# Linear attention in one trunk kernel: half roots of three heads on GpSimd in twelve operations, and output-projection weights from the fourth on split behind the last gates

## The chip, the cores and the metric

The kernel runs on one core of a Trainium2 chip. The metric is device time in microseconds (us): the median of three runs, beside one profiled execution whose trace is quoted throughout. The engines are named as the profile names them: PE is TensorE's matrix multiplies (PEld its weight loads), DVE is VectorE, ACT is ScalarE, POOL is GpSimd, SP is SyncE, which here only issues DMAs.

## What is computed

The reference is a decoder trunk of two layers over 512 tokens and 16 meta tokens, width 1024. Each layer is a feed-forward block, a token mixer, and a second feed-forward block. The mixer of layer 0 is gated linear attention with four heads; the change touches only it. Cut to what matters:

```python
q, k, v, r, lr = split(hn @ w_in)                  # 4 heads, keys 128 wide, values 256 wide
gk = log_sigmoid(lr @ w_gate + b_gate) / 16        # the forget gate
...                                                # chunks of 64: scan, attention, states
o = o_intra + einsum('bhncd,bhndv->bhncv', q_dec, states)
o = rmsnorm(o, g_head) * silu(r)                   # per head and token, over 256 values
return o @ w_out                                   # the output projection
```

## The kernel before

**Order of the work.** PE is the engine that everything is arranged around. A small planner (`Flow`) holds a clock and a heap of jobs. A job is a Python generator that gives out instructions and yields either an estimated delay or another job that it waits for; the main program advances the clock with every matmul that it writes (`mm`, `transpose`, L216). This fixes the order of PE by hand. The order on DVE, ACT and POOL is chosen when the kernel is built, by a scheduler that sees the same estimates and the dependencies. On the chip each engine then runs its own list strictly in order, with semaphores between engines.

**Weights.** Weights arrive as f32 in tiles called `raw` and are split in two parts, a high one made by ACT (L274 and L294, `w<-raw`) and a low one by DVE as a difference (L277 and L295, `w<-raw,w`). `split_unit` (L280) is the job for a plain unit: output projection, among others. Each split tile takes 128x512 on both engines. `L300` adds two raw tiles on DVE for Strassen's products.

**A head of linear attention** is one job, `core(h)`; between its pieces PE works on the input projections of the next head (`x<-x_l0m`), or, in head 2, on the products `a`, `c`, `d` of the gate projection, whose operands are the tiles `zl0m_t` (high part by ACT at L1005, low part by DVE at L1006). In order, a head does this:

- two scans on DVE, L1344 and L1345, from the log gates to `b`
- PE transposes the head's values `V` to tokens by values (`pv`, two groups of four, named pv_0 and pv_1 in the rows of the program's order); ACT copies them out (L1352)
- decays `d`, `f`, `c` (L1361 to L1371) on ACT and DVE, attention, states
- PE computes the output `po` for four blocks of 128 tokens and `pn` for the meta tokens
- ACT squares them and accumulates sums per token (L1434, L1436)
- `half_roots` (L476 to L489, called at L1439): ten DVE instructions on 128x5 numbers, from a sum to half an inverse square root, by an integer guess and two Newton steps. The tile is `half_go`
- ACT scales `po` by the roots, four times `on` (L1443) and once `onm` (L1444)
- PE transposes `on` back (`pt`, L216) and ACT copies the result into `V` (L1453)

The values `V` themselves are written by DVE from PE's projections (L1293, `V<-x,R_l0m`), one instruction of 128x272 and one of 128x256 for each half of a head's values.

**Gates.** Eight jobs `gated(m)` make the operands of the output projection: a tanh on ACT (L1464), two DVE instructions (L1466 and L1471), and `split` into `og`, the high part by ACT (L543) and the low part by DVE (L544). The loop over `plan` spawns them in four pairs. At its last pass but one it raises the cap on loads (`cap`, `prefetch`), and the jobs that split the output projection's eight weight units then run beside the gates. `out_proj` writes PE's products `y<-og,w`.

Of the kernel before, what the change touches and what calls it, by code (L numbers as in the profile page):

```python
# [11 lines left out]
I32 = mybir.dt.int32  # L12
AF = mybir.ActivationFunctionType
ALU = mybir.AluOpType
# [4 lines left out]
KD = 8  # L19
# [7 lines left out]
HEADS = 4  # L27
RSQRT_MAGIC = float(0x5F3759DF)
# [114 lines left out]
def trunk_kernel(ctx: ExitStack, tc, a, out, last_out):  # L143
    nc = tc.nc
    pe, act, dve, pool, sp = nc.tensor, nc.scalar, nc.vector, nc.gpsimd, nc.sync
    flow = Flow()
# [21 lines left out]
    def duo(name):  # L168
        t = pair_tile(name, F32)
        return t[:, 0], t[:, 1]  # L170
# [78 lines left out]
    used, asked, freed, ahead, cap, dma_end = [0], [0], [0], [16], [len(units)], [0.0]  # L249
# [2 lines left out]

    owed, chains = {}, [0]
    rooting, diagonal = set(), []
    building, last_sum, pair_behind, pauses = [], [], {}, []

    def set_ahead(n, slots=None):
        ahead[0], limit[0] = n, slots or n
# [3 lines left out]
    def slot(i):  # L262

        while live[0] + sum(n for j, n in owed.items() if j < i) >= limit[0]:
            yield room[0]
        live[0] += 1
        owed[i] -= 1
# [4 lines left out]
    def split_part(i, raw, m):  # L272
        w = pair_tile(f"w{i}_{len(loaded[i])}")
        high = act.activation(w[:, 0, :m], raw[:, :m], AF.Copy)  # L274
        for x in building:
            after(x.built, high)
        dve.tensor_tensor(w[:, 1, :m], raw[:, :m], w[:, 0, :m].bitcast(F32), op=ALU.subtract)  # L277
        loaded[i].append(w)

    def split_unit(i, raws):  # L280
        yield 2.2
        for raw, m in raws:
            while any((1, KD - 1) not in x.ready for x in building):
                yield 0.5
            yield from slot(i)
            split_part(i, raw, m)
# [50 lines left out]
    def load_unit():  # L337
# [34 lines left out]
        else:  # L372
# [6 lines left out]
            dma_end[0] = max(dma_end[0], flow.clock) + n * 1.5e-3  # L379
            loaded.append([])  # L380
            gen = split_unit(i, raws)
        split_jobs.append(flow.spawn(gen, dma_end[0] - flow.clock))

    def prefetch():
        while len(loaded) < cap[0] and asked[0] + costs[len(loaded)] <= freed[0] + ahead[0]:
            if isinstance(units[len(loaded)], list) and (chains[0] == CHAINS or rooting):
                break
            load_unit()
# [84 lines left out]
        return yy  # L473


    def half_roots(sums, dim, name):  # L476
        n = sums.shape[1]
        t = sm.tile([P, 4, n], F32, tag="half", name=f"half_{name}", bufs=2)
        aa, yy, zz, ww = (t[:, i] for i in range(4))
        dve.tensor_scalar(aa, sums, 1.0 / dim, 1e-6, op0=ALU.mult, op1=ALU.add)  # L480
        dve.tensor_scalar(yy.bitcast(I32), aa.bitcast(I32), -0.5, RSQRT_MAGIC, op0=ALU.mult, op1=ALU.add)
        dve.tensor_tensor(zz, yy, yy, op=ALU.mult)
        dve.tensor_tensor(zz, zz, aa, op=ALU.mult)
        dve.tensor_scalar(ww, zz, 0.375, -1.25, op0=ALU.mult, op1=ALU.add)
        dve.tensor_tensor(ww, ww, zz, op=ALU.mult)
        dve.scalar_tensor_tensor(yy, ww, 1.875, yy, op0=ALU.add, op1=ALU.mult)
        dve.tensor_tensor(zz, yy, yy, op=ALU.mult)
        dve.scalar_tensor_tensor(zz, zz, -0.25, aa, op0=ALU.mult, op1=ALU.mult)
        dve.scalar_tensor_tensor(yy, zz, 0.75, yy, op0=ALU.add, op1=ALU.mult)  # L489
        return yy  # L490

    def rstd(sq, n, dim, half, name, eng=pool, more=0.0):
# [114 lines left out]
    class Residual:  # L607
# [44 lines left out]
        def turn(self, g, sums):  # L652
# [22 lines left out]
            residual(0, 0)  # L675
            total(1)
            f = half_roots(st[:, : n // P], D, self.name)
            residual(0, 1)
            for c in cs:
# [306 lines left out]
    def bring_back_h(kept):  # L986
        H.fresh()
        for q in range(KD // 2):
            rows = slice(2 * q, 2 * q + 2)
            pool.dma_start(H[:, rows, kept], h_kept[:, rows, kept])  # L990
# [262 lines left out]
    def gla(x, finish):  # L1253
        set_ahead(10)
        with tc.tile_pool(name="gp", bufs=1) as gp:
# [82 lines left out]
            def core(h, before):  # L1338
# [86 lines left out]
                sums = sm.tile([P, 5], F32, tag="sums", name=f"sums{h}", bufs=2)  # L1425
# [10 lines left out]
                act.activation(onm, pm[:META, :256], AF.Square, accum_out=sums[:META, 4:5])  # L1436
                mids[h].finish(flow)
                yield SQUARED
                f = half_roots(sums, 256, f"go{h}")  # L1439
                yield DCHAIN  # L1440
                for b in range(4):
                    o = banks[b // 2][:, b % 2 * 256 : b % 2 * 256 + 256]
# [19 lines left out]
            def gated(m):  # L1462
                gs, th = rg[m]
                act.activation(th, gs, AF.Tanh, scale=0.5)  # L1464
                yield 0.8
                dve.scalar_tensor_tensor(gs, th, 1.0, gs, op0=ALU.add, op1=ALU.mult)  # L1466
                yield cores[m // 2]
                yield 0.8 + m % 2 * 1.5
                og[m] = pair_tile(f"og{m}")
                gn = vec[:, V_GN + m % 2 : V_GN + m % 2 + 1]  # L1470
                dve.scalar_tensor_tensor(gs, gs, gn, V[:, m], op0=ALU.mult, op1=ALU.mult)  # L1471
                split(og[m], gs, (0, TOK))
# [9 lines left out]
            for h in range(HEADS):  # L1482
                cores.append(flow.spawn(core(h, [gate] + late + mids[h - 1 : h])))
                if h == 1:
                    flow.spawn(right_factors(x, halves, z, plain, 1.2))
                if h + 1 < HEADS:
                    kk = [("k", h + 1), ("q", h + 1), ("v", 2 * h + 2), ("v", 2 * h + 3)]
                    if h + 2 == HEADS:
                        set_ahead(16, RING)
                        late = x_units(x, 3, L0, lambda i, g, p, kk=kk: evac(*kk[i], g, p))  # L1490
                        plain.finish(flow)
                        late += x_units(x, 1, L0, lambda i, g, p, kk=kk: evac(*kk[3], g, p))
                    else:
                        late = x_units(x, 4, L0, lambda i, g, p, kk=kk: evac(*kk[i], g, p))
            cap[0] = used[0] + len(GLA_PAIRS)
            tiles = Strassen(z, halves, 1)
            jobs = []

            def gating(m):
                rg[m], rg[m + 1] = duo(f"rg{m}"), duo(f"rg{m + 1}")  # L1500
                return Projected(tiles, rg[m][0], rg[m + 1][0])

            def finish_gates(m):
                jobs.extend([flow.spawn(gated(m)), flow.spawn(gated(m + 1))])

            plan = [(lambda m=m: gating(m), lambda m=m: finish_gates(m)) for m in range(0, KD, 2)]

            def begin(i):
                if i == len(plan):
                    return None  # L1510
                t = plan[i][0]()
                t.head()
                return t

            cur = begin(0)
            for i in range(len(plan)):
                cur.body()
                nxt = begin(i + 1)
                cur.tail()
                if i + 2 == len(plan):  # L1520
                    cap[0] = used[0] + KD
                    prefetch()
                plan[i][1]()
                cur = nxt
            bring_back_h(slice(0, TOK))
            flow.wait(*jobs[:6])
            set_ahead(16)
# [321 lines left out]
    x = nxt  # L1849
    nxt, fin = into("l0f1", 0, 3, False, lambda k: gain(0, 4, k), L0)  # L1850
    gla(x, fin)
    x = nxt
    nxt, fin = into("kv", 0, 5, True, lambda k: vec[:, V_KVN + k : V_KVN + k + 1], L0, (1, 1))
# [122 lines left out]
```

## Time and profile before

| | |
|---|---|
| median of 3 runs | 1848.33 us (1847.84 to 1848.58) |
| the profiled execution, its own time | 1847.98 us |
| its span in the trace | 1846.2 us |
| PE busy | 1832.8 us |
| DVE, ACT, POOL busy | 1482.9, 1140.2, 334.0 us |

The span runs from the first to the last recorded instruction; the profiled execution's own time lies 1.8 us above it. A busy row says how long an engine had an instruction in work, whether or not that instruction had to wait for a clock or a port. The rows of a timeline give the start in us from the span's start, the busy time, the engine, the line of the kernel, the operation, the tile written and the tiles read, the shape and the count, and in square brackets the idle time ahead of it with the instruction that ended that idle time. The view by windows gives busy time and count of each engine in a stretch of time, and under PEclk the clock granted to TensorE as a share of the full one. Linear attention's four heads end near 446, 475, 505 and 542 us; the last gates lie near 560 us.

### The profile page before, as it was taken

How to read it: one execution, taken by the hardware profiler on the slowest of the kernel's cores; microseconds unless marked ns; L12 is line 12 of the kernel's file. 1: busy time of each engine (PE TensorE's matmuls, PEld its weight loads, DVE VectorE, ACT ScalarE, POOL GpSimd, SP SyncE). 2: the span in 40 equal slices, each digit the busy share in tenths (PEclk: the TensorE clock that was granted, in tenths of full speed). 3: DMA queues.
4: the chain of work that ended last, by engine and by line, in shares of the span. 5: the costliest groups of instructions: out<-in, count | busy, mean ns of one | idle time of the engine just before them, and what ended most of it. 6: DMA issues, size and time to landing. Idle time of an engine off the chain costs nothing.

```text
span 1846.2 us, 38798 instructions
## 1 busy us (share of the span) xinstructions
PE 1832.8 (99%) x14696; PEld 1776.5 (96%) x14696; DVE 1482.9 (80%) x3047; ACT 1140.2 (62%) x2643; POOL 334.0 (18%) x499
## 2 busy tenths in 40 slices
PE   9999999999999999999999999999999999999998
PEld 9999999999899999999999899999987898999998
DVE  6889888678684788988878789898777678888884
ACT  6666666654566566665665566666667765666564
POOL 2210101321001411010133110212320042111122
PEclk9999999999999999999999999999999999999999
DMA  7756658434234365665853465759430226657681
GB/s 244 196 152 155 167 148 242 158 116 94 50 118 153 105 173 154 154 168 145 256 183 103 139 164 145 180 150 243 159 115 12 69 86 166 160 152 175 155 254 49
DMA packets 146251, 277.45 MB, mean 150 GB/s; under 512 B 16400, under 2 KB 36752, under 8 KB 146064
## 3 DMA queue, kind: packets, MB, share of 16 engines
q1 hardware_dynamic: 114208, 198.15, 33.5%
q0 software_dynamic: 31424, 76.23, 20.7%
q8 instruction: 115, 1.88, 0.4%
q14 instruction: 72, 0.59, 0.1%
q10 hardware_dynamic: 432, 0.59, 0.1%
HBM read 236.05 MB, written 38.34 MB: 149 GB/s over the span
## 4 chain that ended last, share of the span: by engine, by line
PE 91%; DVE 4%; ACT 2%; DMA 1%; issue 1%; SPq 0%; DVEq 0%; ACTq 0%
PE a L204 29%; PE x L204 17%; PE y L204 17%; PE c L204 14%; PE d L204 7%; PE o L204 1%; DVE w L295 1%; PE po L204 1%; ACT s L1696 1%; DVE w_s L295 1%; DMA H<-in_h 1%; DVE raw L300 1%; PE pt L216 1%; ACT w_s L294 0%; DMA raw<-in_w_in 0%
## 5 line engine op out<-in xcount | busy, mean ns | idle before, releaser
L295 DVE TENSOR_TENSOR w_s<-raw,w_s 128x512 fp32r<-128x512 f32 (+1 forms) x432 | 275.1, 647 | 78.8 <-ACT w_s L294 74.5
L294 ACT ACTIVATE w_s<-raw 128x512 fp32r<-128x512 f32 (+1 forms) x432 | 251.0, 593 | 93.0 <-DVE raw L327 49.1
L295 DVE TENSOR_TENSOR w<-raw,w 128x512 fp32r<-128x512 f32 (+1 forms) x324 | 204.2, 646 | 4.1
L353 POOL DMA_DIRECT2D raw<-in_w_in x112 | 104.6, 976 | 449.1 <-DVE w L295 100.5
L294 ACT ACTIVATE w<-raw 128x512 fp32r<-128x512 f32 (+1 forms) x324 | 185.1, 590 | 0.0
L277 DVE TENSOR_TENSOR w<-raw,w 128x512 fp32r<-128x512 f32 x232 | 153.9, 696 | 26.5 <-ACT w L274 24.5
L300 DVE TENSOR_TENSOR raw<-raw,raw 128x512 f32<-128x512 f32 (+1 forms) x264 | 168.0, 636 | 2.2
L274 ACT ACTIVATE w<-raw 128x512 fp32r<-128x512 f32 x232 | 134.5, 620 | 2.4 <-PE y L204 1.1
L204 PE MATMUL y<-hidl0f,w 128*128 128x272 f32 (+1 forms) x960 | 119.4, 285 | 0.0
L204 PEld LDWEIGHTS y<-hidl0f,w 128*128 128x128 f32 x960 | 118.0, 188 | 0.2
L204 PE MATMUL a<-zl0f_t,w_s 128*128 128x264 f32 x864 | 117.3, 285 | 0.0
L204 PE MATMUL y<-hidl1f,w 128*128 128x256 f32 (+1 forms) x768 | 114.9, 310 | 0.0
L204 PE MATMUL a<-zl1f_t,w_s 128*128 128x256 f32 x864 | 113.9, 281 | 0.0
L204 PEld LDWEIGHTS y<-hidl1f,w 128*128 128x128 f32 x768 | 104.9, 188 | 8.5
L538 POOL TENSOR_TENSOR acc_post<-acc_post,sq_post 128x256 f32<-128x256 f32 (+1 forms) x77 | 62.0, 805 | 273.7 <-ACT sq_post L537 270.2
L204 PEld LDWEIGHTS a<-zl0f_t,w_s 128*128 128x128 f32 x864 | 110.4, 188 | 0.0
L1250 POOL DMA_DIRECT2D kept_y<-dn x32 | 36.5, 1141 | 407.1 <-DVE w_s L295 165.3
L204 PEld LDWEIGHTS a<-zl1f_t,w_s 128*128 128x128 f32 x864 | 107.1, 188 | 0.0
L204 PE MATMUL x<-x_l0m,w 128*128 128x256 f32 (+1 forms) x768 | 102.2, 289 | 0.0
L204 PE MATMUL x<-x_l0f,w 128*128 128x256 f32 (+1 forms) x768 | 98.1, 287 | 1.4 <-ACT w L274 0.7
L204 PEld LDWEIGHTS x<-x_l0f,w 128*128 128x128 f32 x768 | 94.8, 189 | 2.7 <-DVE w L277 1.2
L204 PEld LDWEIGHTS x<-x_l0m,w 128*128 128x128 f32 x768 | 95.8, 188 | 1.6 <-issue 0.8
(593 smaller groups left out, 4255.4 us busy)
## 6 DMA issues: line engine op xcount, KB each, us to landing
raw<-in_w_in SPq DMA_DIRECT2D x408, 256.0 KB, 4.2
raw<-in_w_in POOLq DMA_DIRECT2D x112, 256.0 KB, 5.4
raw<-in_w_down SPq DMA_DIRECT2D x128, 192.0 KB, 2.4
raw<-in_gla_in SPq DMA_DIRECT2D x52, 256.0 KB, 3.6
raw<-in_w_last SPq DMA_DIRECT2D x48, 256.0 KB, 4.9
kept_y<-dn POOLq DMA_DIRECT2D x16, 528.0 KB, 8.2
raw<-in_w_out SPq DMA_DIRECT2D x32, 256.0 KB, 2.9
kept_y<-dn POOLq DMA_DIRECT2D x16, 512.0 KB, 8.7
```

The lines of the kernel that those rows point to most:

```text
L204: inst = pe.matmul(o, lhs, rhs, start=start, stop=stop, skip_group_check=onto)
L216: pe.transpose(o, src, ident)
L274: high = act.activation(w[:, 0, :m], raw[:, :m], AF.Copy)
L277: dve.tensor_tensor(w[:, 1, :m], raw[:, :m], w[:, 0, :m].bitcast(F32), op=ALU.subtract)
L294: act.activation(w[:, 0, :m], src, AF.Copy)
L295: dve.tensor_tensor(w[:, 1, :m], src, w[:, 0, :m].bitcast(F32), op=ALU.subtract)
L300: return dve.tensor_tensor(dst, dst, src, op=ALU.add)
L353: added = pool.dma_start(r, src, accum_op=ALU.add)
L538: pool.tensor_tensor(sums[0][:, :n], sums[0][:, :n], t[:, :n], op=ALU.add)
L1250: pool.dma_start(y_sum[:, 2 * self.q : 2 * self.q + 2, o : o + 2 * n], self.y[:, :, : 2 * n], accum_op=ALU.add)
L1696: act.activation(s[:, c], s[:, c], AF.Exp, scale=rc[:, c % 2 : c % 2 + 1], bias=nm[:, c : c + 1], accum_out=den[:, c : c + 1],)
```

## The change

The change has two parts, and both act only in the mixer of layer 0.

1. `half_roots` takes an engine. Heads 0, 1 and 2 pass GpSimd, head 3 still passes DVE. On GpSimd each of the three `scalar_tensor_tensor` steps becomes a `tensor_scalar` and a `tensor_tensor`, arranged so that there are twelve instructions instead of ten.
2. A dictionary `unit_behind` names units whose job waits for another job before it splits. When the cap for the output projection is raised, units 3 to 7 of its eight (the fourth on) are put behind a new job `gated_all`, which ends when all eight `gated` jobs have ended.

```diff
     def split_unit(i, raws):
         yield 2.2
+        if i in unit_behind:
+            yield unit_behind.pop(i)
         for raw, m in raws:
...
-    def half_roots(sums, dim, name):
+    def half_roots(sums, dim, name, eng=dve):
...
+        if eng is dve:
+            dve.scalar_tensor_tensor(yy, ww, 1.875, yy, op0=ALU.add, op1=ALU.mult)
+            dve.tensor_tensor(zz, yy, yy, op=ALU.mult)
+            dve.scalar_tensor_tensor(zz, zz, -0.25, aa, op0=ALU.mult, op1=ALU.mult)
+            dve.scalar_tensor_tensor(yy, zz, 0.75, yy, op0=ALU.add, op1=ALU.mult)
+        else:
+            eng.tensor_scalar(ww, ww, 1.875, None, op0=ALU.add)
+            eng.tensor_tensor(yy, yy, ww, op=ALU.mult)
+            eng.tensor_tensor(zz, yy, yy, op=ALU.mult)
+            eng.tensor_tensor(zz, zz, aa, op=ALU.mult)
+            eng.tensor_scalar(zz, zz, -0.25, 0.75, op0=ALU.mult, op1=ALU.add)
+            eng.tensor_tensor(yy, yy, zz, op=ALU.mult)
         return yy
...
-                f = half_roots(sums, 256, f"go{h}")
+                f = half_roots(sums, 256, f"go{h}", pool if h + 1 < HEADS else dve)
...
+            gated_all = Job(None)
+
+            def all_gated():
+                for j in jobs:
+                    yield j
+                gated_all.finish(flow)
...
                 if i + 2 == len(plan):
+                    unit_behind.update((j, gated_all) for j in range(used[0] + 3, used[0] + KD))
                     cap[0] = used[0] + KD
                     prefetch()
...
+            flow.spawn(all_gated())
             bring_back_h(slice(0, TOK))
```

The lines of the changed kernel stand ten further on behind `half_roots`: L1443 before is L1453 after, L1006 is L1016. The order of PE's 4255 rows and of SP's rows is the same in both programs, apart from names. POOL's list gains the 36 rows of the three chains, each at its head's place. DVE's list loses 30 rows; DVE and ACT lists are also re-sorted at a few places within linear attention, and nowhere else.

The first place is ACT in head 2. `on` and `onm` are the scalings that read the roots; `zl0m_t_6607` (6613 in the changed kernel) is the fourth of the gate projection's operand tiles of this stretch. Before:

```order
L1005 ACTIVATE zl0m_t_6584<-xsl0m_5737 128x528
L294 ACTIVATE w_11_6590<-raw_0_6520 128x512
L1005 ACTIVATE zl0m_t_6607<-xsl0m_5738 128x528
L1390 ACTIVATE dec_6832<-b_6631 128x4
L1352 ACTIVATE vt_6634<-pv_0_6635 128x4x128
L1361 ACTIVATE d_6682<-b_6631 128x528
L1443 ACTIVATE on_6493<-po_0_6490,half_go_6546 128x256 x2
L1443 ACTIVATE on_6493<-po_1_6491,half_go_6546 128x256 x2
L1444 ACTIVATE onm_6494<-pn_6492,half_go_6546 16x256
L1352 ACTIVATE vt_6634<-pv_1_6650 128x4x128
```

And in the changed kernel, where the five scalings have moved ahead of the fourth `zl0m_t`, of `dec`, of the copy of pv_0 and of `d`:

```order
L1015 ACTIVATE zl0m_t_6590<-xsl0m_5737 128x528
L296 ACTIVATE w_11_6596<-raw_0_6524 128x512
L1453 ACTIVATE on_6497<-po_0_6494,half_go_6550 128x256 x2
L1453 ACTIVATE on_6497<-po_1_6495,half_go_6550 128x256 x2
L1454 ACTIVATE onm_6498<-pn_6496,half_go_6550 16x256
L1015 ACTIVATE zl0m_t_6613<-xsl0m_5738 128x528
L1400 ACTIVATE dec_6838<-b_6637 128x4
L1362 ACTIVATE vt_6640<-pv_0_6641 128x4x128
L1371 ACTIVATE d_6688<-b_6637 128x528
```

The second place is DVE at the same time. `V_3<-x_0` and `V_3<-x_1` write the values that PE's pv_1 transposes. Before:

```order
L295 TENSOR_TENSOR w_11_6590<-raw_0_6520,w_11_6590 128x512
L483 TENSOR_TENSOR half_go_6546<-half_go_6546 128x5
L1006 SCALAR_TENSOR_TENSOR zl0m_t_6607<-xsl0m_5738,zl0m_t_6607 128x528
L484 TENSOR_SCALAR half_go_6546<-half_go_6546 128x5
L1344 SCALAR_TENSOR_TENSOR b_6631<-resets,ls_5498 128x528
L485 TENSOR_TENSOR half_go_6546<-half_go_6546 128x5
L1345 SCALAR_TENSOR_TENSOR b_6631<-resets,ls_5498 128x528
L486 SCALAR_TENSOR_TENSOR half_go_6546<-half_go_6546 128x5
L1293 TENSOR_TENSOR V_3_6532<-x_0_6535,R_l0m 128x272
L487 TENSOR_TENSOR half_go_6546<-half_go_6546 128x5
L1293 TENSOR_TENSOR V_3_6532<-x_1_6536,R_l0m 128x256
```

And in the changed kernel, where the fourth `zl0m_t` stands between the two scans and so ahead of both writes of `V_3`, and the addition of two raw tiles has moved up:

```order
L297 TENSOR_TENSOR w_11_6596<-raw_0_6524,w_11_6596 128x512
L302 TENSOR_TENSOR raw_0_6524<-raw_0_6524,raw_3_6527 128x512
L1354 SCALAR_TENSOR_TENSOR b_6637<-resets,ls_5498 128x528
L1016 SCALAR_TENSOR_TENSOR zl0m_t_6613<-xsl0m_5738,zl0m_t_6613 128x528
L1355 SCALAR_TENSOR_TENSOR b_6637<-resets,ls_5498 128x528
L1303 TENSOR_TENSOR V_3_6536<-x_0_6539,R_l0m 128x272
L1303 TENSOR_TENSOR V_3_6536<-x_1_6540,R_l0m 128x256
```

The third place is DVE at the last two gates. `og` are the gated values, `w_0` and `w_1` the halves of a unit of the output projection's weights. Before:

```order
L1471 SCALAR_TENSOR_TENSOR rg_7117<-rg_7117,vec,V_3_6532 128x528
L277 TENSOR_TENSOR w_0_7330<-raw_0_7179,w_0_7330 128x512
L277 TENSOR_TENSOR w_1_7333<-raw_512_7181,w_1_7333 128x512
L544 TENSOR_TENSOR og_7354<-rg_7116,og_7354 128x528
L277 TENSOR_TENSOR w_0_7358<-raw_0_7183,w_0_7358 128x512
L277 TENSOR_TENSOR w_1_7361<-raw_512_7185,w_1_7361 128x512
L277 TENSOR_TENSOR w_0_7376<-raw_0_7226,w_0_7376 128x512
L277 TENSOR_TENSOR w_1_7379<-raw_512_7228,w_1_7379 128x512
L544 TENSOR_TENSOR og_7385<-rg_7117,og_7385 128x528
```

And in the changed kernel, where both `og` follow the gates at once and the weights come behind them; ACT's list has the same shift:

```order
L1481 SCALAR_TENSOR_TENSOR rg_7123<-rg_7123,vec,V_3_6536 128x528
L554 TENSOR_TENSOR og_7354<-rg_7122,og_7354 128x528
L554 TENSOR_TENSOR og_7373<-rg_7123,og_7373 128x528
L277 TENSOR_TENSOR w_0_7377<-raw_0_7185,w_0_7377 128x512
L277 TENSOR_TENSOR w_1_7380<-raw_512_7187,w_1_7380 128x512
L277 TENSOR_TENSOR w_0_7383<-raw_0_7189,w_0_7383 128x512
```

More of the change, by code (lines that the diff above doesn't have):

```diff
@@ L254, in trunk_kernel @@
     rooting, diagonal = set(), []
-    building, last_sum, pair_behind, pauses = [], [], {}, []
+    building, last_sum, pair_behind, unit_behind, pauses = [], [], {}, {}, []
     def set_ahead(n, slots=None):
@@ L479, in half_roots @@
         aa, yy, zz, ww = (t[:, i] for i in range(4))
[L480 to L489, printed above, removed]
+        eng.tensor_scalar(aa, sums, 1.0 / dim, 1e-6, op0=ALU.mult, op1=ALU.add)
+        eng.tensor_scalar(yy.bitcast(I32), aa.bitcast(I32), -0.5, RSQRT_MAGIC, op0=ALU.mult, op1=ALU.add)
+        eng.tensor_tensor(zz, yy, yy, op=ALU.mult)
+        eng.tensor_tensor(zz, zz, aa, op=ALU.mult)
+        eng.tensor_scalar(ww, zz, 0.375, -1.25, op0=ALU.mult, op1=ALU.add)
+        eng.tensor_tensor(ww, ww, zz, op=ALU.mult)
+        if eng is dve:
[6 more added lines that the diff above has]
+            eng.tensor_tensor(yy, yy, ww, op=ALU.mult)
+            eng.tensor_tensor(zz, yy, yy, op=ALU.mult)
+            eng.tensor_tensor(zz, zz, aa, op=ALU.mult)
+            eng.tensor_scalar(zz, zz, -0.25, 0.75, op0=ALU.mult, op1=ALU.add)
+            eng.tensor_tensor(yy, yy, zz, op=ALU.mult)
         return yy
```

## The prediction, made before the changed kernel ran

> **What bounds the kernel now.** I read the page first: busy shares, then the chain that ended last.
>
> ```profile
> PE 1832.8 (99%) x14696; PEld 1776.5 (96%) x14696; DVE 1482.9 (80%) x3047; ACT 1140.2 (62%) x2643; POOL 334.0 (18%) x499
> PE 91%; DVE 4%; ACT 2%; DMA 1%; issue 1%; SPq 0%; DVEq 0%; ACTq 0%
> ```
>
> PE is busy for 99% of the span and carries 91% of the chain. Freeing DVE is worth nothing by itself: only a stretch where PE stands, or runs slowly, can give time back. The waits of PE name two that the change can touch:
>
> ```profile
> PE pt L216 <- ACT on L1443: 1.2, 2, 0.8
> PE y L204 <- DVE og L544: 0.9, 1, 0.9
> ```
>
> The timeline of PE places them, and the windows show the clock around them:
>
> ```profile
> 445.27 1.43 PE L216 MATMUL pt<-ident,on 128*128 128x128 f32 x4 [0.41 <-ACT on L1443]
> ...
> 474.85 0.60 PE L216 MATMUL pt<-ident,on 128*128 128x128 f32 x4
> ...
> 501.96 0.60 PE L216 MATMUL pv<-ident,V 128*128 128x128 f32 x4
> 503.35 1.42 PE L216 MATMUL pt<-ident,on 128*128 128x128 f32 x4 [0.79 <-ACT on L1443]
> ...
> 565.14 1.09 PE L204 MATMUL y<-og,w 128*128 128x272 f32 x7 [0.90 <-DVE og L544]
> ```
>
> ```profile
> 443.58:446.99 3.41, 2.89 (x17) 1.89 (x16) 3.41 (x10) 2.25 (x7) 0.86 (x1) 1.00 0.52 103
> 501.60:505.01 3.41, 2.51 (x15) 1.49 (x13) 1.75 (x6) 3.02 (x8) 0.00 (x0) 1.00 0.07 12
> 505.01:508.43 3.42, 3.42 (x15) 2.91 (x16) 1.27 (x4) 2.62 (x6) 0.00 (x0) 0.50 0.00 0
> 563.04:566.45 3.41, 2.51 (x20) 2.29 (x19) 3.25 (x6) 1.31 (x4) 0.00 (x0) 1.00 0.71 245
> ```
>
> Unhindered, four transposes take 0.60 us (501.96, 474.85). Behind ACT's scalings they take 1.42 and 1.43. So head 0 loses 0.41 + 0.83 = 1.24 us, head 1 nothing, head 2 0.79 + 0.82 = 1.61 us, the gates 0.90. In head 2 the granted clock then falls to 0.50 for one window of 3.42 us, which costs PE half of it, 1.71. The window before it held 15 matmuls; one with 17 (head 0) and one with 20 (gates) were followed by no drop. Head 2 thus loses 3.32 us. All that the change can reach is 1.24 + 3.32 + 0.90 = 5.46 us, 0.3% of the time.
>
> **Part one: the roots on POOL.** It takes ten small operations off DVE in three heads and puts twelve on POOL.
>
> ```profile
> L480 DVE TENSOR_SCALAR half_go<-sums x4: 164/169/172, 438.5 to 532.7; 128x5 f32<-128x5 f32 x4
> ...
> L489 DVE SCALAR_TENSOR_TENSOR half_go<-half_go x4: 144/155/159, 444.5 to 538.5; 128x5 f32<-128x5 f32 x4
> ```
>
> On DVE head 0's chain runs from 438.5 to 444.65 (444.5 and the last one's 0.15), since a long instruction stands between each two. What POOL takes is shown by the same kind of chain elsewhere, once free and once beside DVE:
>
> ```profile
> 372.87 0.19 POOL L452 TENSOR_SCALAR yv_l0m<-av_l0m 68x4 int32<-68x4 int32 x1 [3.14 <-ACT av_l0m L451]
> ...
> 375.69 0.20 POOL L470 TENSOR_TENSOR yv_l0m<-yv_l0m,zv_l0m 68x4 f32<-68x4 f32 x1
> ```
>
> ```profile
> 993.68 0.51 POOL L457 TENSOR_SCALAR wv_kv<-zv_kv 128x2 f32<-128x2 f32 x1
> ...
> 997.88 0.52 POOL L470 TENSOR_TENSOR yv_kv<-yv_kv,zv_kv 128x2 f32<-128x2 f32 x1
> ```
>
> ```profile
> 993.45 4.90 DVE L277 TENSOR_TENSOR w<-raw,w 128x512 fp32r<-128x512 f32 x8
> ```
>
> Free, eleven operations start within 2.82 us, 0.28 apart: twelve take 3.4. Beside eight subtractions of DVE, 4.90 / 8 = 0.61 apart, eight take 997.88 - 993.68 = 4.20 over seven steps, 0.60 each: one per DVE instruction. Twelve then take 7.2. DVE lost nothing to them.
>
> The Trainium skill ("SBUF — State Buffer", Who interferes with whom) calls the shared port pair an exclusive lock and says that issue order decides who blocks. By that, a POOL operation that comes first would hold DVE, by up to its 0.20 us; the rows show DVE at its usual pace, and so I add nothing. By the rule, head 2's chain below would end up to some 0.6 us later and the forecast would be about 1849.4.
>
> Head 0: starting at 438.5, the chain ends at 441.9 free and at 445.7 blocked throughout. DVE there is full of long instructions, some reading PSUM, with one gap; I take 444.9, near the blocked end: 0.25 us later than 444.65, so **+0.25** (-1.24 to +1.1).
>
> Head 1: the chain can start when DVE's did, 466.83.
>
> ```profile
> 466.83 0.17 DVE L480 TENSOR_SCALAR half_go<-sums 128x5 f32<-128x5 f32 x1 [0.82 <-ACT onm L1436]
> ...
> 470.11 0.15 DVE L489 SCALAR_TENSOR_TENSOR half_go<-half_go 128x5 f32<-128x5 f32 x1
> ```
>
> Free it ends at 470.2, blocked at 474.0. DVE stood idle ahead of it and has only four long instructions within it, so about five operations run free and seven blocked: 466.83 + 1.4 + 4.2 = 472.4. The scalings need 1.6 us (below), PE wants them at 474.85 and, at its own pace, takes the last 0.4 later; so up to 473.1 nothing is lost: **0** (to +0.9). This 0.7 us of slack hides it.
>
> Head 2 is where the order moved. The rows of DVE and ACT before:
>
> ```profile
> 493.96 0.78 DVE L1293 TENSOR_TENSOR V<-x,R_l0m 128x272 f32<-128x272 f32 x2 [5.13 <-PE x L204]
> 494.66 0.68 DVE L295 TENSOR_TENSOR w<-raw,w 128x512 fp32r<-128x512 f32 x1
> ...
> 498.01 0.70 DVE L1006 SCALAR_TENSOR_TENSOR zl0m_t<-xsl0m,zl0m_t 128x528 fp32r<-128x528 f32 x1
> 498.63 0.16 DVE L484 TENSOR_SCALAR half_go<-half_go 128x5 f32<-128x5 f32 x1
> 498.70 1.25 DVE L1344 TENSOR_TENSOR_SCAN b<-resets,ls 128x528 f32<-128x528 f32 x1
> ...
> 501.14 0.44 DVE L1293 TENSOR_TENSOR V<-x,R_l0m 128x272 f32<-128x272 f32 x1
> ...
> 501.56 0.42 DVE L1293 TENSOR_TENSOR V<-x,R_l0m 128x256 f32<-128x256 f32 x1
> ...
> 502.57 0.16 DVE L489 SCALAR_TENSOR_TENSOR half_go<-half_go 128x5 f32<-128x5 f32 x1
> ```
>
> ```profile
> 493.48 0.18 ACT L1436 ACTIVATION_READ_ACCUMULATOR onm<-pn 16x1 f32 x1
> ...
> 496.50 0.65 ACT L1005 ACTIVATE zl0m_t<-xsl0m 128x528 fp32r<-128x528 f32 x1
> ...
> 502.83 1.57 ACT L1443 ACTIVATE on<-po,half_go 128x256 f32<-128x256 f32 x4 [0.39 <-DVE half_go L489]
> 504.27 0.45 ACT L1444 ACTIVATE onm<-pn,half_go 16x256 f32<-16x256 f32 x1
> 504.62 0.57 ACT L1352 ACTIVATE vt<-pv 128x512 f32<-128x512 f32 x1
> ```
>
> POOL starts at 493.75. Until 494.66 DVE reads PSUM, and I let four operations run free; then come six long DVE instructions (two w, three zl0m_t, one addition) at some 0.65, with one operation each, to 498.55; the scan of 1.25 holds one more, and the last follows: the roots are ready at 500.3 (497.1 wholly free; 501.0 if one more is missed), against 502.73 before.
>
> That is earlier, and yet not what PE gets. In the new order ACT's fourth zl0m_t stands behind the five scalings, and DVE's low part of it ahead of the second scan and of both writes of V_3, which PE needs for pv_1, ahead of pt. So: ACT starts `on` at 500.4; the next instruction follows after 504.62 - 502.83 = 1.79, at 502.2, and takes 0.65; DVE's zl0m_t starts at 502.9 (before: 498.01), the second scan 0.62 later, the first write 1.17 after that (1.25 less the overlap of 0.08 that 498.01, 0.70 and 498.63 show), at 504.7; the second write starts 0.36 later and ends at 505.5. Of the idle time that DVE gets meanwhile nothing reaches PE. PE wants pv_1 at 501.96 and stands until 505.5: 3.54 us. The scalings are then long done, and pt runs unhindered.
>
> The window from 501.60 then holds some three matmuls, against 15 before, and a half clock follows: from 505.5 to 508.43 PE loses half of 2.93, 1.46 us. Head 2 loses 5.0 instead of 3.32: **+1.7**; after rounding for transposes of pv_1 that need the first write alone, I take **+1.5**. Bounds: with the roots at 497.1 nothing is lost, -3.3; at 501.0, +2.4.
>
> POOL's own DMA issues behind the chains start at most some 2 us later than before and the tiles are wanted tens of us later; I price that at nothing.
>
> **Part two: the gates.** DVE's second `og` stands behind four weight halves:
>
> ```profile
> 561.98 2.49 DVE L277 TENSOR_TENSOR w<-raw,w 128x512 fp32r<-128x512 f32 x4
> 564.39 0.70 DVE L544 TENSOR_TENSOR og<-rg,og 128x528 fp32r<-128x528 f32 x1
> ```
>
> In the new order it follows the first at about 561, three us before PE asks (565.14 - 0.90 = 564.24). The wait goes. What is late next would be the weights: ten halves at 0.6 follow from 561.7 and end by 567.8; PE has three units in hand, 24 matmuls for each half of the tokens by its order, so that far more than 50 stand between 564.24 and the fourth unit, and at 0.16 us each (1.09 / 7 in the row of 565.14) that lies beyond 572. **-0.95** (-1.06 to 0).
>
> **Sum:** 0.25 + 0 + 1.5 - 0.95 = +0.8 us on the profiled execution's 1847.98 (span 1846.2 and 1.8 around it; 0.35 under the median): **1848.8**.
>
> **The rivals.**
>
> - *The order bites less, faster.* POOL runs its chains nearly free: roots at 441.9 and 497.1; the scalings and zl0m_t are done before 499.6, V_3 is written by 502, and every stall goes: 1.24 + 3.32 + 0.90 = 5.46 less, 1842.5. For it: the free chain at 372.87. Against: the pace at 993.68, and DVE's full list in head 0. 0.12.
> - *Head 0 falls under the clock as well, slower.* Its window held 17 matmuls without a drop, head 2's 15 with one. If POOL's chain ends at 445.3 or later, PE stands 0.65 longer, the window loses several more, and a half clock of 1.71 us follows: 1848.8 + 0.4 + 1.7 = 1850.9; with head 2's roots at 501.0 also, 1851.8 to 1852.3. It decides from about 0.25 us of further delay, if the windows lie as before. 0.22.
> - *No half clock in head 2.* PE's 3.5 us fall across two windows with matmuls in both, and neither is followed by a drop: 1848.8 - 1.46 = 1847.3. The Trainium skill ("TensorE: Matmul & The Clock Gate", Part 1) gives the half clock after an idle window of about 3.4 us; read strictly, no window here is wholly idle, and the forecast would be that 1847.3. The rows speak against that strict reading: the drop at 505.01 followed a window with 15 matmuls in it. 0.12.
> - *The second part does nothing for PE*, because another wait stands right behind og at 564.24: 1849.75. The order shows og moved. 0.04.
>
> **How the numbers follow.** The forecast has 0.50 and spans 1847.6 to 1849.8 with the bounds of head 0 and of the roots' time around its middle. 0.2% (3.7 us, below 1844.6 or above 1852.0) is about what a measurement of this kernel can tell from no change. Faster takes the first rival, 0.12; slower the upper part of the second and a remainder for two half-clock windows in a row, 0.11; the rest, 0.77, lies within. For 8 in 10 I leave out the first rival and the uppermost part of the second: 1845.2 to 1851.6.
>
> **What would show it.** In the changed profile: POOL's `half_go` operations some 0.6 apart beside long DVE instructions; PE's wait on `on` in head 2 gone and one on V (L1303) at pv, of about 3.5 us, followed by a window at 0.50; ACT's fourth zl0m_t of head 2 behind `on`; head 1 without a stall; no wait of `y` on `og`. The prediction falls if the waits on `V` at pv are under 2 us, or if POOL's operations run at 0.28 throughout.

## The result, and the profile after

The changed kernel takes 1852.12 us (median of 13 runs, 1848.53 to 1855.67); the kernel before, run 13 times beside it, 1846.31 us (1842.91 to 1848.58). The ratio is 1.0031, with a 95% interval from 1.0021 to 1.0040: 5.8 us slower by the medians, 3.9 to 7.4 by the interval. The forecast was 0.8 us slower and its range ended at 1851.6. The profiled execution that the prediction worked from, 1847.98 us, lies high among those 13.

The first lines of the page of the changed kernel's profiled execution (1855.67 us, the longest of its 13) show the span and the busy times:

```profile
span 1853.9 us, 38798 instructions
...
PE 1837.3 (99%) x14696; PEld 1780.3 (96%) x14696; DVE 1480.3 (80%) x3017; ACT 1138.9 (61%) x2643; POOL 352.0 (19%) x535
```

DVE lost 2.6 us of work and POOL gained 18.0 for 36 instructions: 0.5 us each, not 0.2. PE is busy 4.5 us longer with the same instructions, so it ran slowly somewhere. The waits of PE, which before named `pt` with 0.8 at most and `y` behind `og` with 0.9, now begin so:

```profile
PE pv L216 <- DVE V L1303: 2.7, 1, 2.7
PE pt L216 <- ACT on L1453: 1.9, 1, 1.9
PE x L204 <- DVE w L277: 1.3, 4, 0.3
```

The wait of `y` on `og` has gone from the list. `pv` waits for V, a wait that was not there. `pt` has one wait in place of two, and it is more than twice as long. The timeline of PE has them in place, with head 1 between them; the times in brackets are the idle time ahead of a row:

```profile
446.92 1.42 PE L216 MATMUL pt<-ident,on 128*128 128x128 f32 x4 [1.86 <-ACT on L1453]
...
479.58 1.42 PE L216 MATMUL pt<-ident,on 128*128 128x128 f32 x4
...
510.43 1.08 PE L216 MATMUL pv<-ident,V 128*128 128x128 f32 x4 [2.69 <-DVE V L1303]
511.31 1.06 PE L216 MATMUL pt<-ident,on 128*128 128x128 f32 x4
```

Head 0 waits 1.86 instead of 0.41. Head 1 now takes 1.42 for four transposes instead of 0.60, which means that they follow ACT's scalings one by one. Head 2's wait has moved from pt to pv and grown to 2.69. The view by windows shows what followed the waits of heads 0 and 2; its columns are PE, PEld, DVE, ACT and POOL busy with their counts, then the granted clock, and last the share and rate (GB/s) of DMA:

```profile
444.88:448.29 3.41, 1.44 (x6) 0.55 (x4) 0.58 (x2) 1.90 (x6) 2.15 (x5) 1.00 0.00 0
448.29:451.70 3.41, 3.41 (x15) 2.97 (x15) 2.23 (x6) 3.41 (x9) 0.00 (x0) 0.50 0.50 77
451.70:455.11 3.41, 3.41 (x17) 3.41 (x17) 3.12 (x6) 3.17 (x7) 0.00 (x0) 0.50 0.10 35
506.32:509.73 3.41, 1.43 (x13) 1.21 (x10) 1.65 (x2) 1.72 (x5) 0.48 (x1) 1.00 0.52 77
509.73:513.14 3.41, 2.71 (x12) 2.37 (x12) 2.21 (x5) 3.15 (x8) 0.00 (x0) 0.50 0.00 0
513.14:516.56 3.42, 3.42 (x16) 2.90 (x16) 1.75 (x5) 1.00 (x2) 0.00 (x0) 0.50 0.00 0
```

In this execution each of the two waits is followed by two windows at half clock. In the profiled execution of before, head 0 had none and head 2 one. The changed kernel's profiled execution is the longest of its 13 and has more such windows than most: its mean granted clock is 0.994, against 0.9964 over all 13.

Why the roots come late is in POOL's own rows. Head 0 from its fifth long one on, and the middle of head 1:

```profile
441.87 0.52 POOL L487 TENSOR_TENSOR half_go<-half_go 128x5 f32<-128x5 f32 x1
442.47 1.53 POOL L494 TENSOR_SCALAR half_go<-half_go 128x5 f32<-128x5 f32 x1
444.09 0.20 POOL L495 TENSOR_TENSOR half_go<-half_go 128x5 f32<-128x5 f32 x1
444.37 1.16 POOL L496 TENSOR_TENSOR half_go<-half_go 128x5 f32<-128x5 f32 x1
...
474.01 0.58 POOL L494 TENSOR_SCALAR half_go<-half_go 128x5 f32<-128x5 f32 x1
474.68 3.23 POOL L495 TENSOR_TENSOR half_go<-half_go 128x5 f32<-128x5 f32 x1
477.99 0.19 POOL L496 TENSOR_TENSOR half_go<-half_go 128x5 f32<-128x5 f32 x1
```

One operation on 128x5 numbers took 3.23 us. DVE at that time:

```profile
473.79 0.70 DVE L1025 TENSOR_TENSOR xsl0m<-xsl0m 128x528 f32<-128x528 f32 x1
474.42 0.41 DVE L1367 COPY vm<-pm 16x256 f32<-16x256 f32 x1
474.75 0.69 DVE L1016 SCALAR_TENSOR_TENSOR zl0m<-xsl0m,zl0m 128x528 fp32r<-128x528 f32 x1
475.37 0.69 DVE L1372 TENSOR_TENSOR d<-d,qk 128x528 f32<-128x528 f32 x1
...
477.16 0.69 DVE L1025 TENSOR_TENSOR xsl0m<-xsl0m 128x528 f32<-128x528 f32 x1
477.78 0.42 DVE L1301 TENSOR_TENSOR qk<-x,R_l0m 128x272 f32<-128x272 f32 x1
```

The POOL operation of 474.01 began within the 0.70 us instruction of 473.79 and ended 0.1 after it, as the prediction had it: one per DVE instruction. The next one began at 474.68, under the short copy of 474.42 that reads PSUM. It ended at 477.91, behind all six instructions from 474.75 to 477.85, and just after `qk`, which reads PSUM, had begun. It missed every boundary between.

### The profile page after: what moved, and what is told of

The parts are those of the page before. It is cut to its first block, busy times and chain, and to the rows that moved or that the text cites. A ratio compares the mean times of both kernels' runs of the same rounds, so it can differ in the third digit from the quotient of the medians.

```text
span 1853.9 us, 38798 instructions
## 1 busy us (share of the span) xinstructions
PE 1837.3 (99%) x14696; PEld 1780.3 (96%) x14696; DVE 1480.3 (80%) x3017; ACT 1138.9 (61%) x2643; POOL 352.0 (19%) x535
## 4 chain that ended last, share of the span: by engine, by line
PE 92%; DVE 3%; ACT 2%; issue 1%; DMA 1%; POOL 1%; SPq 0%; DVEq 0%; ACTq 0%; POOLq 0%
PE a L204 29%; PE y L204 17%; PE x L204 17%; PE c L204 14%; PE d L204 7%; PE o L204 1%; PE po L204 1%; DVE w L297 1%; ACT s L1714 1%; PE pt L216 1%; DMA H<-in_h 1%; DVE raw L302 1%; DVE w_s L297 1%; ACT w_s L296 0%; PE ps L204 0%
```

## The experiments

Theory A: each head that has its roots on POOL gets them later than PE needs them, PE stands, and half-clock windows follow; in head 2 it is the place of one instruction in ACT's list that does it. Rivals are that the re-sorted lists of DVE and ACT cost by themselves (B), that the second part costs (C), and that POOL is late in head 2 whatever the order (D). Theory E and rival F concern why a POOL operation is held. Each experiment has 11 or 12 runs. All ratios are to the kernel before on the same chip, 35 runs with a median of 1846.4 in the first four experiments and of 1846.8 in the last four; microseconds are worked out from the ratio.

**The second part alone.**

```diff
-                f = half_roots(sums, 256, f"go{h}", pool if h + 1 < HEADS else dve)
+                f = half_roots(sums, 256, f"go{h}", dve)
```

> Only the second part: the fourth and later weight units of the output projection wait for the gates; the roots stay on DVE in all heads. Theory A (the loss comes from the roots on POOL being late, PE standing for them, and the half-clock windows that follow): the wait of y on og, 0.90 us, goes and nothing replaces it: about 0.9 us faster than before, and the three heads as before. Rival B (the loss is made by the lists of DVE and ACT being re-sorted, not by POOL's pace) says the same of this run, since nothing in the heads is re-sorted here. Rival C (the second part itself costs): 1 to 3 us slower.

Measured: 1844.59 us, ratio 0.9993 (0.9985 to 1.0002), 1.3 us faster with an interval from 2.8 faster to 0.4 slower. The waits of PE in this run name `pt` as before and no `y` behind `og`:

```profile
PE pt L216 <- ACT on L1453: 1.2, 2, 0.8
PE y L204 <- ACT so L553: 1.1, 1, 1.1
PE busy L1806 <- DVE eps L1858: 1.0, 1, 1.0
```

C falls. The gain fits the expected 0.9; the interval holds zero, so that the gain is shown by the wait that has gone rather than by the time alone.

**Roots of one head at a time on POOL, without the second part.** The edit, for head 0; heads 1 and 2 likewise:

```diff
-                    unit_behind.update((j, gated_all) for j in range(used[0] + 3, used[0] + KD))
...
-                f = half_roots(sums, 256, f"go{h}", pool if h + 1 < HEADS else dve)
+                f = half_roots(sums, 256, f"go{h}", pool if h == 0 else dve)
```

> Roots of head 0 alone on POOL, second part left out. Theory A: the chain ends near 446.4 as in the changed kernel, PE's gap ahead of pt is about 2.1 us instead of 0.6, and one or two windows of half clock follow in some executions: 1.5 us slower without them, up to 4.9 with two, so some 3 in the median. Rival B: the list of DVE and ACT is re-sorted in head 0 as well, but only behind the roots; it would cost nothing, 0.

Measured: 1849.13 us, ratio 1.0013 (1.0004 to 1.0022), 2.4 us slower. PE's wait on `on` is 1.9 at its longest, and in the profiled execution one window at half clock follows. Besides the three places shown with the change there is a fourth: in head 0 ACT's `f<-b` and `dec` stand behind the five scalings too (442.07 and 442.61 before, 448.18 and 448.72 in the changed kernel). In this run DVE stood 4.01 us for the `zl0m_t` behind them, but PE's one wait in head 0 is the one on `on`.

> Roots of head 1 alone on POOL, second part left out. ACT's and DVE's lists keep their order here but for one instruction. Theory A: one POOL operation waits through several DVE instructions, the chain takes about 7.5 us instead of 3.4, the transposes pt start late by 0.1 and run 0.36 apart: 1.0 us slower. Rival B: nothing is re-sorted, so no change, 0.

Measured: 1848.72 us, ratio 1.0011 (1.0003 to 1.0020), 2.0 us slower. One POOL operation took 3.22 us, under the same copy; PE's four transposes of head 1 took 1.42. In its trace that is 0.95 us (0.82 of slower pace, and 0.13 by which they start later against the products ahead of them); no half-clock window lies there in the profiled execution. The other 1 us isn't in this trace; the interval is 0.6 to 3.7.

> Roots of head 2 alone on POOL, second part left out. Theory A: pv_1 waits about 2.7 us for V behind the fourth zl0m_t, instead of pt's 0.8 and its slow pace; +1.4 us, and one more half-clock window in some executions, 1.7: between 1.4 and 3.1 slower. Rival B: the whole loss is here, 5 to 6 us slower.

Measured: 1848.60 us, ratio 1.0015 (1.0005 to 1.0024), 2.8 us slower (0.9 to 4.4); the wait of pv on V is 3.0 us, and in the profiled execution one window at half clock follows, as in before. B falls as the account of the whole: head 1, where only one instruction of ACT moved, costs about as much as the others, and head 2 is not the whole loss. (In head 2 the order is the cause, as the next run shows.) The three heads and the gates add up to 2.4 + 2.0 + 2.8 - 1.3 = 5.9 us; the whole change costs 5.8. Each of the four is known to some 1.7 us either way, so that an agreement this close is in part luck.

**Head 2 with ACT's order of before at that one place.** The estimate of the roots' time is raised, so that the scheduler puts the scalings later; the time to the transposes is cut by as much, and PE's order stays:

```diff
-                yield DCHAIN
+                yield DCHAIN + (1.2 if h == 2 else 0)
...
-                yield SCALED + (BESIDE / 2 if h else 0)
+                yield SCALED + (BESIDE / 2 if h else 0) - (1.2 if h == 2 else 0)
```

> Roots of head 2 alone on POOL, second part left out, and the estimate of the roots' time 1.2 us longer (the time until the transposes that much shorter): PE's order and POOL's stay, and ACT's fourth zl0m_t now stands ahead of the five scalings, as it did before the change. Theory A: head 2's loss came from that one place in ACT's list; the roots are ready at about 500.1, the scalings done at 502, V written by 501.9, and pv and pt do not wait: before's wait of 0.8 and the slow pace go too. 1.6 us faster than before without counting the clock, up to 3.3 where the half-clock window goes with it. Rival D (POOL is the trouble in head 2 as well, whatever ACT's order): as slow as with head 2 alone on POOL, some 2.7 us over before.

Measured: 1845.18 us, ratio 0.9990 (0.9981 to 0.9998), 1.8 us faster than before, and 4.6 faster than the run with head 2 alone on POOL. The lists of PE and POOL are the same in these two. ACT's differ in the one place, and DVE's follow: the low part of the fourth `zl0m_t` now stands ahead of both scans, and the addition of two raw tiles behind them, still ahead of V. The timeline of its ACT, and then of its PE:

```profile
496.14 0.65 ACT L1015 ACTIVATE zl0m_t<-xsl0m 128x528 fp32r<-128x528 f32 x1
501.05 1.57 ACT L1453 ACTIVATE on<-po,half_go 128x256 f32<-128x256 f32 x4 [4.26 <-POOL half_go L499]
```

```profile
501.95 0.66 PE L216 MATMUL pv<-ident,V 128*128 128x128 f32 x4 [0.18 <-ACT on L1453]
502.68 0.66 PE L216 MATMUL pt<-ident,on 128*128 128x128 f32 x4
```

The roots came at 501.02, not at 500.1 as expected, since the two scans, now back to back, held two operations for 1.03 and 1.06 us. Even so pv waited only 0.18 and pt nothing. D falls. In the changed kernel the same rows of ACT read:

```profile
505.62 1.57 ACT L1453 ACTIVATE on<-po,half_go 128x256 f32<-128x256 f32 x4 [3.59 <-POOL half_go L499]
507.06 0.45 ACT L1454 ACTIVATE onm<-pn,half_go 16x256 f32<-16x256 f32 x1
507.42 0.63 ACT L1015 ACTIVATE zl0m_t<-xsl0m 128x528 fp32r<-128x528 f32 x1
```

There ACT stood 3.59 us for POOL with zl0m_t behind it, whose input had long been ready, and DVE stood 2.76 for zl0m_t.

**Head 1 without the copy that reads PSUM.** The copy `vm` of the next head goes to ACT:

```diff
-                dve.tensor_copy(vm[:META], pm[:META, :256])
+                (act.activation(vm[:META], pm[:META, :256], AF.Copy) if h == 2
+                 else dve.tensor_copy(vm[:META], pm[:META, :256]))
```

> Roots of head 1 alone on POOL, second part left out, and the copy of the next head's meta values (vm) made by ACT instead of DVE, so that no instruction of DVE that reads PSUM stands within the chain. Theory E: the 3.2 us that one POOL operation waited came from its start under that copy, just ahead of a run of long DVE instructions, and a POOL operation that starts within such an instruction gets its turn at its end: no operation over 0.8 us, the chain about 5 us instead of 7.5, PE not delayed: within 0.3 us of before. Rival F (any operation may be held for as long as DVE has no gap): one operation still takes 2 us or more and the time stays some 2 us over before.

Measured: 1846.65 us, ratio 1.0003 (0.9994 to 1.0012): 0.6 us slower with an interval from 1.1 faster to 2.2 slower, no difference from before to be seen. The time by itself does not separate this from the 2.0 (0.6 to 3.7) with the copy on DVE; the rows do. POOL's rows from the eighth operation on, to be set beside the 3.23 us above:

```profile
470.15 0.49 POOL L495 TENSOR_TENSOR half_go<-half_go 128x5 f32<-128x5 f32 x1
470.72 0.54 POOL L496 TENSOR_TENSOR half_go<-half_go 128x5 f32<-128x5 f32 x1
471.33 0.54 POOL L497 TENSOR_TENSOR half_go<-half_go 128x5 f32<-128x5 f32 x1
471.96 0.47 POOL L498 TENSOR_SCALAR half_go<-half_go 128x5 f32<-128x5 f32 x1
472.51 0.54 POOL L499 TENSOR_TENSOR half_go<-half_go 128x5 f32<-128x5 f32 x1
```

The chain took 466.96 to 473.05, 6.1 us instead of 7.5. I had expected some 5: from the fifth operation on, nearly each had a DVE instruction to wait for. But no operation was held for more than 0.67, and PE was not delayed: its four transposes took 0.60 again. F falls for this chain.

**The gates with head 2 mended, heads 0 and 1 on DVE.** This is the second part with the two lines of the experiment on head 2's order.

> The second part as in the changed kernel, roots of head 2 alone on POOL with ACT's fourth zl0m_t ahead of the scalings, heads 0 and 1 on DVE. Theory A: the two gains add, 0.9 to 1.3 from the gates and 1.6 to 3.3 from head 2: 2.5 to 4.5 us faster than before, a version that beats both. Rival D: gates' gain less 2.7, so about 1.5 us slower.

Measured: 1841.40 us, ratio 0.9974 (0.9966 to 0.9983), 4.8 us faster than before (3.1 to 6.3): the fastest of this study. It is more than the 1.3 + 1.8 = 3.1 us of the two runs by themselves, though the interval holds that. The mean granted clock of its runs is 0.9989, against 0.9974 for before; whether all of that is the edits' doing is open.

**The whole change, mended at both places** (the order in head 2; `vm` by ACT for heads 1 and 2, whose copies lie in the chains of heads 0 and 1).

> The whole change, with two amendments: in head 2 ACT's fourth zl0m_t ahead of the scalings, and the vm copies within the chains of heads 0 and 1 made by ACT. Theory A with E: head 0's chain loses the 1.0 us of the operation that waited behind the copy and ends near 445.3, 0.7 later than before, so that head 0 still costs some 0.7 us and now and then a half-clock window; head 1 costs nothing; head 2 and the gates gain: about 2 to 3 us faster than before, 8 faster than the change. Rival D and F: as the change, some 5 to 6 us slower than before.

Measured: 1843.22 us, ratio 0.9982 (0.9974 to 0.9991), 3.3 us faster than before and, by the two ratios, 9 below the change. Head 0's chain:

```profile
442.12 0.58 POOL L494 TENSOR_SCALAR half_go<-half_go 128x5 f32<-128x5 f32 x1
...
444.58 0.25 POOL L499 TENSOR_TENSOR half_go<-half_go 128x5 f32<-128x5 f32 x1
```

It ends at 444.83, no operation over 0.72; PE still waits 0.7 for `on` in head 0, against 0.41 with the roots on DVE, and in the profiled execution one window at half clock follows. So on POOL head 0 gains nothing over DVE even then. The version without heads 0 and 1 has the lower median; by their intervals the two cannot be told apart.

## Why the prediction was wrong

- **Head 0, forecast +0.25 (-1.24 to +1.1).** This is the step that failed first: "Twelve then take 7.2", one POOL operation per DVE instruction, as the blocked end. The chain took 438.72 to 446.35, 7.6 us, beyond that end, though several of its operations ran free. Two were held across whole runs of DVE instructions, 1.53 and 1.16 us. PE's wait grew by 1.45 us (1.86 against 0.41), and the half clock, which the sum had left to a rival, followed in the profiled executions: 2.4 us measured for this head alone (0.7 to 4.1).
- **Head 1, forecast 0 (to +0.9), with 0.7 us of slack.** It failed in the same way: the sum of five free and seven blocked operations gave 5.6 us; one operation took 3.23 alone and the chain 7.5. The slack was gone; 0.95 us in the trace, 2.0 measured. The slack itself was added up wrong, on the safe side: 474.85 + 0.4 - 1.6 is 473.65, not 473.1. The roots came at 479.01; the products ahead of the transposes end 4.60 later than before, so that this is 474.4 by the times of before. "Head 1 without a stall" is the listed sign that failed outright.
- **Head 2, forecast +1.5.** The mechanism was right, and shown by the run that undoes only the order. The wait on V was 2.69 where I had 3.54. I counted 1.46 us for one window at half clock; two followed in the profiled execution of the changed kernel, one with head 2 alone. 2.8 measured, with an interval (0.9 to 4.4) that holds the 1.5.
- **Gates, forecast -0.95.** Right: the wait of 0.90 is gone, and 1.3 was measured with an interval that holds it. The forecast gave no row for the 0.05 beyond the wait.
- **The rival that came closest** was head 0 under the clock as well, 1850.9 to 1852.3, with 0.22. By its own account it needed some 0.25 us of delay beyond the forecast 0.25; PE's wait grew by 1.45. That its span holds the measured 1852.12 is in part luck: it priced at most 4.3 us over a base that lay high, had nothing for head 1, and the change cost 5.8.
- **The base.** The profiled execution that I built on, 1847.98, lies 1.2 to 1.7 us above the medians of before (1846.3, 1846.4 and 1846.8). Ahead of its last microseconds its trace has three windows at half clock: the one in head 2, and two from 1406.13 to 1412.96, behind waits of `y` in layer 1 that the change doesn't touch. That pair stands, near the same work, in six of the ten traces on record, of before and of the changed kernel among them, and is missing in four. PE is busy all through it, so that it costs half of 6.83, some 3.4 us by estimate, in the executions that have it. My range, built on one execution, was at once too high at its middle and too narrow for what the clock adds from one execution to the next (before: 1842.9 to 1850.2 over all its runs).
- **Standing or slow.** Every execution lists its mean granted clock, to three places. Over the first 35 runs of before, the time falls on a line with about 1.4 us for each 0.001 of mean clock, from 1843.0 at the full clock; over the second 35 it is 1.6, from 1842.6; over the 13 runs of the change 1.5, from 1846.6. The means are 0.9978 for the first 35 and 0.9964 for the change. By these lines, as an estimate, 3.6 to 4.0 of the 5.8 us are there at full clock, and some 2 come from more half-clock windows. In the traces, PE's waits and slower transposes account for 1.45 + 0.95 + 1.08 - 0.90 = 2.6 us of the first part (for head 2, 2.69 less before's 1.61); the rest of it is open.

## What to carry to other kernels

When a chain of small operations moves to GpSimd beside a busy DVE, look in DVE's list for instructions that read PSUM just ahead of runs of long ones: there an operation was held for the whole run in three cases here, 3.2 us at the longest, and in one like case it was not. An instruction that waits for such a chain should stand behind everything on its engine that PE needs sooner; moving one `zl0m_t` ahead of five scalings was worth 4.6 us here. Where PE is the bound, a wait of two or three microseconds was at times paid twice here, once as the wait and again in half-clock windows.

## What the runs showed of the hardware

- A POOL operation that began while a long two-input DVE instruction ran was released 0.05 to 0.11 us after that instruction's end in the changed kernel's three chains. The three that were held longest in the changed kernel (1.53, 1.16, 3.23 us) all began under a DVE instruction reading PSUM, 0.14 to 0.21 us before it ended, with two-input instructions back to back behind it, and were released at the end of that run. The single heads' runs repeat them (1.53, 1.16, 3.22), and taking the copy off DVE took the 1.53 and the 3.23 away. It is not the whole rule: in head 2 an operation that began under the write of V, 0.14 before that ended, with long instructions behind it, took 0.19. The 1.16 went too in the run mended at both places, with its `qk` still on DVE, as the operations fell at other moments. What tells the cases apart is open: the runs do not separate the reading of PSUM from the moment at which an operation begins. The Trainium skill ("SBUF — State Buffer", Who interferes with whom) says that a DVE instruction with two SBUF inputs contends with a GpSimd instruction that reads SBUF, over a port pair that is an exclusive lock. That agrees with the operations of 0.5 us, held to the end of one instruction; that one can be held across six, for 3.23, it does not say.
- A scan of 1.25 us on DVE held a POOL operation to its end (1.02 to 1.07 us, in the changed kernel and in the runs with head 2's order mended), like a two-input instruction.
- The half clock came after windows that were idle in part only. Leaving out the last microseconds, the windows ahead of it in the ten traces held 5 (head 2 alone, 501.61) to 18 matmuls (head 1 alone, 1403.81), with PE busy for 0.45 to 2.60 of 3.41 us. Neither figure gives a threshold: in the run mended at both places a window with 15 matmuls and 2.19 us busy (1400.08) was followed by no drop, and one with 14 and 2.60 (444.35) was. So the prediction's 15 against 17 was no rule. The half clock lasted one window in some executions and two in others, the second also with PE busy all through the first. What decides between one and two is open. The Trainium skill ("TensorE: Matmul & The Clock Gate", Part 1) gives the half clock after one idle window; here a partly idle one was enough.
